# A two-layer decoder trunk on one core: a planner that counts held operand loads, new ranks, and indexer products on 128 rows

## The chip, the core and the metric

The kernel runs on one core of one Trainium2 chip. A core has a matrix engine (PE; its weight loads, PEld, are listed apart), a vector engine (DVE), a scalar engine (ACT), a general engine (POOL), and queues that issue DMA; here SP's queue issues nearly all of them. Each engine runs its instructions in the order in which they were written down and waits on semaphores for the others. The metric is the device time of one execution in microseconds (us).

## What is computed

Two layers, then a final norm, on x of 512 tokens by 1024 channels in float32:

```python
h = rmsnorm(x, norm_w); p = split_cols(h @ w_in)      # w_in: 1024 x 3380
o_a = dsa_mixer(...)   # indexer: 8 heads of 32, relu, weighted sum, top 128 keys; then softmax attention, 4 heads of 64
o_b = nsa_mixer(...)   # compressed blocks, selected blocks and window: three softmaxes, gated
o_c = shortconv_mixer(...); o_d = pool_mixer(...)
mixed = concat(silu(gates) * (o_a, o_b, o_c, o_d))
x = x + mixed @ w_out                                 # after two layers: rmsnorm(x, final_norm_w)
```

The indexer's score of query t and key s is the sum over 8 heads of `relu(qi . ki) * wi`; the compressed branch adds a table `pe_cmp` (32 x 64 per layer) to the tokens of each block before its product.

## The kernel before

Tokens are in four tiles of 128 (`i` = 0 to 3). Every float32 operand of a large product is split into a high part in a rounded format (names `wh`, `hT`, `ph`, `mT` ...) and a rest (`wl`, `pl`, the second `hT` and `mT`), and three products are summed: high by high, high by rest, rest by high. Weights come in parts of 256 rows by up to 384 columns: a DMA into a staging tile `st` (four buffers; two early groups use the tiles `ws`, which are not shared), ACT or DVE writes `wh`, POOL or DVE writes `wl` (`load_w`).

The stages of a layer: `norm_tile` (mean of squares, `pow` on POOL, scaling on DVE, transposes on PE, `hT`); the projections by token tile, `group_a` (360 columns), `group_idx` (256, the indexer's queries `qiT`), `group_bk` (268), `group_bq` (320); `compress`, gates, attention (`att_a`, `att_b`), top-k on DVE (`topk`: 16 pairs of MAX8 and MATCH_REPLACE8 a tile), convolution and pooling, and the output projection (`out_tile`, `store`), whose last column group carries the mean of squares of the next norm.

`group_idx` ends in eight products a tile, `s<-kiT,qiT`: 96 rows hold high, high and rest of the query against high, rest and high of the key. ACT applies relu in the PSUM bank `s` (two banks), DVE adds into `acc`, and a bank is free for the next product when DVE has read it.

Nothing is issued as it is written. Every call is recorded as an `Op` (line 529 of the profile is the one line that later issues them all, so every row of the trace has L529), and `Tape.schedule` puts them in order by list scheduling with its own estimate of each duration (`cost`): for each engine it takes, among the operations that could start soonest, the one whose stage has the lowest number in the table `RANK`; `earliest` says when an operation could start. Queue orders, SP's too, are a result of this. 40 transposes of `ident` at the start (`warm`) are recorded as work with no consumer.

Of the kernel before, what the change touches and what calls it, by code (L numbers as in the profile page):

```python
# [18 lines left out]
P = 128  # L19
T = 512  # L20
# [158 lines left out]
class Op:  # L179
    __slots__ = ("eng", "name", "args", "kw", "outs", "ins", "before", "left", "behind", "dur", "occ", "seen",  # L180
                 "tiles", "start", "ready", "num", "locks", "moves", "stage", "rank", "group", "load", "part")


class Engine:
# [42 lines left out]
class Tape:  # L227
# [37 lines left out]
    def record(self, eng, name, args, kw):  # L265
# [22 lines left out]
        for views, writes in ((op.ins, False), (op.outs, True)):  # L288
            for v in views:
# [3 lines left out]
                if adds:  # L293
                    for (a, b, had), other in v.tile.groups.items():
                        if a == r0 and r1 < b and bits & ~had == 0:
                            op.group = other
                            op.before[other[0].num] = other[0]
                            op.part = True
# [1103 lines left out]
```

## Time and profile before

| | us |
|---|---|
| median of three runs (lowest, highest) | 547.8 (547.03, 548.99) |
| the profiled execution, its own time | 548.15 |
| its span, first to last instruction | 546.4 |
| between the two | 1.75 |

| engine | busy us | share of the span | instructions |
|---|---|---|---|
| PE | 528.5 | 97% | 3139 |
| PEld | 455.9 | 83% | 3139 |
| DVE | 403.9 | 74% | 1139 |
| ACT | 320.7 | 59% | 797 |
| POOL | 320.4 | 59% | 504 |

Busy time of PE is the union of its matmuls, whose ends are modelled and overlap: a PE that is shown busy need not be at its peak, but a PE that is shown idle has nothing. "[2.11 <-ACT wh]" in a row of the timeline is idle time of that engine ahead of the instruction and what ended it. In the views by line, the first number behind the bar is the group's busy time in us, the second the mean of one in ns, the third the idle time ahead of it.

### The profile page before, as it was taken

The numbers are of one execution on the slowest core, as the hardware profiler recorded it, in microseconds if no ns is written. First come the engines' busy times: TensorE is split into PE (matmuls) and PEld (weight loads), VectorE is DVE, ScalarE is ACT, GpSimd is POOL, SyncE is SP. The second block draws the span as 40 slices with busy tenths as digits, with TensorE's granted clock in tenths as the row PEclk, the third lists the DMA queues.
The fourth block names the chain that finished last, engine by engine and source line by source line (L and its number), as shares of the span: only waits on it lengthen the run. The fifth ranks groups of instructions, "written<-read, shape, count | busy, mean of one in ns | idle before, by whom it ended". The sixth has DMA issues, their size and how long they took to land.

```text
span 546.4 us, 9871 instructions
## 1 busy us (share of the span) xinstructions
PE 528.5 (97%) x3139; PEld 455.9 (83%) x3139; DVE 403.9 (74%) x1139; ACT 320.7 (59%) x797; POOL 320.4 (59%) x504
## 2 busy tenths in 40 slices
PE   7979999999999999999999999999999999999995
PEld 7978987677788887899999999777788877788895
DVE  3737799998998878751266568999997968777433
ACT  5358856544486666743255788634366666666433
POOL 6665653373748587636666766347276686574632
PEclk9999999999999999999999999999999999999998
DMA  8761230471224012225642532167142113020304
GB/s 278 195 201 48 50 79 20 130 199 39 60 57 105 3 40 59 78 88 170 191 154 80 132 86 55 39 165 164 40 106 68 50 30 87 0 79 22 104 1 155
DMA packets 70100, 50.65 MB, mean 93 GB/s; under 512 B 19224, under 2 KB 64416, under 8 KB 70048
## 3 DMA queue, kind: packets, MB, share of 16 engines
q1 hardware_dynamic: 69344, 49.38, 32.5%
q10 hardware_dynamic: 704, 0.64, 0.4%
q8 instruction: 25, 0.41, 0.3%
q14 instruction: 27, 0.22, 0.1%
HBM read 45.81 MB, written 4.19 MB: 92 GB/s over the span
## 4 chain that ended last, share of the span: by engine, by line
PE 73%; DVE 9%; DMA 6%; ACT 4%; issue 3%; POOL 3%; SPq 1%; ACTq 0%; POOLq 0%; DVEq 0%
PE mm L529 53%; PE tr L529 8%; PE s L529 6%; PE pv L529 5%; DVE acc L529 4%; DMA st<-in_w_in_dram 3%; ACT wh L529 2%; DVE m L529 2%; POOL pb L529 1%; DMA ws<-in_w_in_dram 1%; POOL wl L529 1%; SPq L529 1%; DMA st<-in_w_out_dram 1%; ACT qiT L529 1%; DVE qb L529 1%
## 5 line engine op out<-in xcount | busy, mean ns | idle before, releaser
L529 POOL TENSOR_TENSOR wl<-st,wh 128x384 fp32r<-128x384 f32 (+4 forms) x188 | 173.5, 952 | 84.3 <-ACT wh L529 69.2
L529 PE MATMUL mm<-hT,wh 128*128 128x512 f32 x544 | 182.2, 403 | 1.4 <-ACT wh L529 1.1
L529 PEld LDWEIGHTS mm<-hT,wh 128*128 128x128 f32 x544 | 100.0, 189 | 20.3 <-ACT wh L529 3.9
L529 PE MATMUL mm<-wh,hT 128*128 128x360 f32 (+3 forms) x480 | 107.0, 308 | 3.0 <-ACT wh L529 2.9
L529 PE MATMUL mm<-hT,wl 128*128 128x512 f32 x272 | 106.8, 403 | 0.0
L529 ACT ACTIVATE wh<-st 128x768 fp32r<-128x768 f32 (+4 forms) x92 | 70.9, 777 | 49.1 <-PE mm L529 25.6
L529 PE MATMUL mm<-wh,mT 128*128 128x384 f32 (+1 forms) x384 | 92.7, 324 | 1.2 <-ACT wh L529 0.5
L529 PEld LDWEIGHTS mm<-wh,hT 128*128 128x128 f32 x480 | 79.5, 189 | 4.8 <-ACT wh L529 3.6
L529 PE MATMUL mm<-wl,hT 128*128 128x360 f32 (+3 forms) x240 | 70.4, 306 | 0.0
L529 PEld LDWEIGHTS mm<-wh,mT 128*128 128x128 f32 x384 | 65.9, 189 | 4.9 <-ACT wh L529 1.2
L529 ACT ACTIVATE pb<-pb,mn 128x512 f32<-128x512 f32 (+3 forms) x96 | 53.3, 557 | 15.1 <-DVE mn L529 14.4
L529 PE MATMUL mm<-wl,mT 128*128 128x384 f32 (+1 forms) x192 | 60.4, 323 | 0.0
L529 PEld LDWEIGHTS mm<-hT,wl 128*128 128x128 f32 x272 | 51.0, 188 | 10.2 <-POOL wl L529 1.8
L529 POOL TENSOR_SCALAR pb<-pb,rs,gt 128x512 f32<-128x512 f32 (+2 forms) x48 | 38.8, 824 | 25.8 <-DVE rs L529 12.2
L529 DVE MATCH_REPLACE8 acc<-m,acc 128x384 f32<-128x384 f32 (+2 forms) x96 | 51.7, 541 | 0.0
L529 ACT ACTIVATE ph<-tr 128x512 fp32r<-128x512 f32 (+1 forms) x68 | 38.1, 595 | 23.2 <-PE tr L529 21.1
L529 DVE MAX8 m<-acc 128x8 f32<-128x384 f32 (+2 forms) x96 | 51.2, 549 | 0.3
L529 DVE TENSOR_TENSOR pl<-tr,ph 128x512 fp32r<-128x512 f32 x60 | 39.9, 684 | 14.6 <-ACT ph L529 11.8
L529 PE MATMUL tr<-ident,pb 128*128 128x128 f32 x240 | 45.7, 275 | 0.9 <-POOL pb L529 0.8
L529 PEld LDWEIGHTS mm<-wl,hT 128*128 128x128 f32 x240 | 44.3, 189 | 0.1
L529 DVE TENSOR_TENSOR x<-mm,x 128x256 f32<-128x256 f32 (+2 forms) x32 | 12.7, 421 | 40.8 <-PE mm L529 40.0
L529 PEld LDWEIGHTS tr<-ident,pb 128*128 128x128 f32 x240 | 30.7, 140 | 10.9 <-POOL pb L529 4.8
(163 smaller groups left out, 915.0 us busy)
## 6 DMA issues: line engine op xcount, KB each, us to landing
st<-in_w_in_dram SPq DMA_DIRECT2D x104, 128.0 KB, 2.6
st<-in_w_in_dram SPq DMA_DIRECT2D x28, 256.0 KB, 2.9
st<-in_w_out_dram SPq DMA_DIRECT2D x16, 384.0 KB, 3.3
x<-in_x_dram SPq DMA_DIRECT2D x16, 256.0 KB, 4.6
st<-in_w_in_dram SPq DMA_DIRECT2D x7, 320.0 KB, 4.6
st<-in_w_out_dram SPq DMA_DIRECT2D x8, 256.0 KB, 2.8
x1d<-x SPq DMA_DIRECT2D x8, 256.0 KB, 3.0
x<-x1d SPq DMA_DIRECT2D x8, 256.0 KB, 2.8
```

The source lines that it names most:

```text
L529: getattr(self.engines[op.eng].real, op.name)(*[real(a) for a in op.args], **{k: real(v) for k, v in op.kw.items()})
```

## The change

- The planner: the field `part` and the rule that let a smaller product join an open accumulation group go. A new field `late` (45 for a transpose, 109 for 128 columns of weights) is added to every wait of a PE operation, on its operands and on its buffers. The spacing of two loads no longer enters `earliest`; it is applied to the operation that was chosen. Some estimates for PE and POOL change.
- `RANK` has new numbers throughout, so the order of every engine changes.
- `group_idx`: the queries are written twice side by side (512 columns instead of 256), rotated twice, and turned by four transposes instead of two; two ACT and two DVE instructions of 64 x 512 write `qiT` in place of eight ACT and four DVE instructions of 32 x 256. The products take 128 rows.
- `mean_sq`: the last column piece of a tile is reduced on DVE (a product and sum with the earlier pieces as its start), where ACT squared and POOL added: 12 pieces in all.
- `compress`: `pe` is loaded turned, by two DMAs of single elements, where a DMA, a PE transpose and an ACT copy made it.
- `pv`: the product with `pl` is one of 512 columns by 128, where it was two of 256 columns by 64; its place is free within the sum. `cmp_pv` and `vc` have 128 rows instead of 96, the added ones zero.

```diff
 RANK = [
-    3, 2, 577, 31, 1, 0, 0, 41, 54, 50, 52, 46, 4, 53, 12, 19, 0, 47, 11, 51, 14, 0, 17, 60, 106, 83, 0, 100, 0,
+    1, 0, 577, 3, 5, 0, 576, 28, 38, 2, 6, 4, 29, 34, 27, 42, 0, 30, 39, 22, 40, 0, 45, 43, 44, 12, 0, 32, 0,
...
                 if adds:
-                    for (a, b, had), other in v.tile.groups.items():
-                        if a == r0 and r1 < b and bits & ~had == 0:
-                            op.group = other
-                            op.before[other[0].num] = other[0]
-                            op.part = True
-                    if op.group is None:
-                        op.group = v.tile.groups.setdefault((r0, r1, bits), [])
-                        if kw["stop"]:
-                            op.before.update((o.num, o) for o in op.group if o.part)
+                    op.group = v.tile.groups.setdefault((r0, r1, bits), [])
...
             op.load = 109 * int(np.prod(op.args[1].shape[1:])) / 128
+            op.late = 45 if op.name == "transpose" else op.load
...
-                        op.occ *= 0.55
+                        op.occ *= 0.6
+                        op.seen += 600
...
-                op.dur = 262 + 0.84 * n
+                op.dur = 262 + 0.84 * n + (75 if sum(isinstance(a, View) for a in op.args) > 3 else 0)
...
-                op.dur = 180 + 2.15 * n
+                op.dur = 180 + (1.7 if len(op.ins) == 2 and op.ins[0].tile is op.ins[1].tile else 2.15) * n
...
-                    s = max(s, pl.free[k])
+                    s = max(s, pl.free[k] + op.late)
                 elif pl.pool.name == "pp":
-                    s = max([s] + [at for other, at in t.used.items() if other != e])
-            if e == "PE" and before is not None:
-                s = max(s, before.start + op.load * (2 if before.start < COLD else 1))
+                    s = max([s] + [at + op.late for other, at in t.used.items() if other != e])
...
             e = op.eng
+            if e == "PE" and last[e] is not None:
+                s = max(s, last[e].start + op.load * (2 if last[e].start < COLD else 1))
...
-                o.ready = max(o.ready, s + (occ if e == "PE" else op.dur + OWN[e]) if o.eng == e else s + op.seen)
+                o.ready = max(o.ready, s + (occ if e == "PE" else op.dur + OWN[e]) if o.eng == e else s + op.seen + o.late)
...
-    def mean_sq(xp, acc):
+    def mean_sq(xp, acc, last=True):
...
-        S.activation(junk[:, : xp.shape[-1]], xp, AF.Square, accum_out=ss)
-        G.tensor_scalar(ss, ss, 1.0 / DM, EPS if acc is None else acc, op0=OP.mult, op1=OP.add)
+        if last and acc is not None:
+            V.tensor_tensor_reduce(out=junk[:, : xp.shape[-1]], in0=xp, in1=xp, scale=1.0 / DM, scalar=acc, op0=OP.mult,
+                                   op1=OP.add, accum_out=ss)
+            return ss
+        S.activation(junk[:, : xp.shape[-1]], xp, AF.Square, scale=DM**-0.5, accum_out=ss)
+        G.tensor_scalar(ss, ss, 1.0, EPS if acc is None else acc, op0=OP.mult, op1=OP.add)
...
-            z = wk.tile([P, 384], F32, name=nm("z"), tag="ph", bufs=3)
-            z3 = z[:, :256].rearrange("p (h d) -> p h d", d=ID)
-            S.activation(z[:, :256], ps[:, :256], AF.Copy)
-            rope(V, z3, IH, 4, tab[:, TB32 + 16 * i : TB32 + 16 * i + 16])
+            z = wk.tile([P, T], F32, name=nm("z"), tag="ph", bufs=3)
+            q3 = ps[:, :256].rearrange("p (h d) -> p h d", d=ID)
+            S.activation(z.rearrange("p (h s d) -> p h s d", s=2, d=ID), q3[:, :, None, :].to_broadcast([P, IH, 2, ID]), AF.Copy)
+            rope(V, z.rearrange("p (h d) -> p h d", d=ID), 2 * IH, 4, tab[:, TB32 + 16 * i : TB32 + 16 * i + 16])
...
-            for h in range(4):
-                src = pq[ID * h : ID * (h + 1), 0 : 2 * P].rearrange("p (b t) -> p b t", b=2)
-                q = qiT[h // 2][:, h % 2]
-                for r in range(2):
-                    S.activation(q[r * ID : (r + 1) * ID], src, AF.Copy)
-                lo(V, q[2 * ID : 3 * ID], src, q[0:ID])
+            for c in range(4):
+                PE.transpose(pq[:, c * P : (c + 1) * P], z[:, c * P : (c + 1) * P], ident)
+            p3 = pq.rearrange("p (c t) -> p c t", c=4)
+            qiT = [wk.tile([P, 4, P], F32R, name=nm("qiT"), tag="big", bufs=BIG) for _ in range(2)]
+            for e in range(2):
+                r, o = slice(HD * e, HD * e + HD), slice(HD - HD * e, P - HD * e)
+                S.activation(qiT[e][r], p3[r], AF.Copy)
+                lo(V, qiT[e][o], p3[r], qiT[e][r])
...
-                PE.matmul(ps[:, :n], qiT[h % 4 // 2][: 3 * ID, h % 2, h // 4, :], kiT[: 3 * ID, :n], start=True, stop=True)
+                PE.matmul(ps[:, :n], qiT[h % 2][:, h // 2, :], kiT[:, :n], start=True, stop=True)
...
-            pet = sm.tile([16, 2, HD], F32, name=nm("pet"), tag="pet", bufs=1)
-            SP.dma_start(pet, pe_cmp[l].rearrange("(s t) d -> t s d", s=2))
-            pt = bank("tr", 3)
-            PE.transpose(pt[:, 0:16], pet.rearrange("t s d -> t (s d)"), ident[0:16, 0:16])
             pe = sm.tile([P, 16], F32, name=nm("pe"), tag="pe", bufs=1)
-            S.activation(pe, pt[:, 0:16], AF.Copy)
+            for s in range(2):
+                SP.dma_start(pe[HD * s : HD * s + HD], pe_cmp[l, 16 * s : 16 * s + 16, :].rearrange("t d -> d t"))
...
-                end = last and k == i
-                if not end:
-                    PE.matmul(po, vt(k), ph, start=first and k == 0, stop=False)
-                if end and i == 0:
-                    PE.matmul(po, vt(k), pl, start=True, stop=False)
-                else:
-                    for c in (slice(0, T // 2), slice(T // 2, T)):
-                        PE.matmul(po[0:HD, c], vt(k)[:, 0:HD], pl[:, c], start=False, stop=False)
-                if end:
-                    PE.matmul(po, vt(k), ph, start=False, stop=True)
+                PE.matmul(po, vt(k), ph, start=first and k == 0, stop=False)
+                PE.matmul(po, vt(k), pl, start=False, stop=last and k == i)
...
-                PE.transpose(pt[0:96, h * P : (h + 1) * P], es[:, h, :], ident)
+                PE.transpose(pt[:, h * P : (h + 1) * P], es[:, h, :], ident)
...
-                    ms[i] = mean_sq(xo, ms[i])
+                    ms[i] = mean_sq(xo, ms[i], e == DM)
```

**Place one: SP's queue in the first 32 us.** `ws_230` before and `ws_216` in the change stage the four parts of the indexer's weights, `ws_254` those of `group_bk`; `x` are token tiles (the later ones for the residual), `pe` and `pet` the table `pe_cmp`. Before, from the last constant to the last part of the indexer's weights:

```order
L529 DMA psc<-in_pool_scale_dram 128x2x1
L529 DMA st_405<-in_w_in_dram 128x2x256
L529 DMA st_405<-in_w_in_dram 128x2x64
L529 DMA pet_426<-in_pe_cmp_dram 16x2x64
L529 DMA ws_230<-in_w_in_dram 128x2x256
L529 DMA g_450<-in_norm_w_dram 128x512
L529 DMA x_461<-in_x_dram 128x512
L529 DMA x_468<-in_x_dram 128x512
L529 DMA x_476<-in_x_dram 128x512
L529 DMA x_484<-in_x_dram 128x512
L529 DMA ws_230<-in_w_in_dram 128x2x256
```

Now, from the last part of the first weights on:

```order
L523 DMA st_189<-in_w_in_dram 128x2x320
L523 DMA st_189<-in_w_in_dram 128x2x40
L523 DMA tab<-in_table_dram 128x258
L523 DMA ws_216<-in_w_in_dram 128x2x256 x4
L523 DMA ws_254<-in_w_in_dram 128x2x268 x4
L523 DMA st_277<-in_w_in_dram 128x2x256
L523 DMA st_277<-in_w_in_dram 128x2x64
L523 DMA pe_290<-in_pe_cmp_dram 64x16x1 x2
```

The indexer's four parts have moved from between the constants and the residual's tiles (the last as SP's 51st DMA) to right behind the table (SP's 16th to 19th).

**Place two: POOL and DVE at the start.** On POOL, the mean of squares of the first token tile (`ss`), the `pow` with `mhalf`, and the rests of the first weights; before:

```order
L529 TENSOR_SCALAR ss_137<-ss_137 128x1
L529 TENSOR_SCALAR ss_163<-ss_163,ss_137 128x1
L529 TENSOR_TENSOR wl_175<-st_90,wh_168 128x360
L529 TENSOR_TENSOR ss_163<-ss_163,mhalf 128x1
L529 TENSOR_TENSOR wl_216<-st_102,wh_186 128x360
```

and now:

```order
L523 TENSOR_SCALAR ss_138<-ss_138 128x1
L523 TENSOR_TENSOR ss_162<-ss_162,mhalf 128x1
L523 TENSOR_SCALAR ss_177<-ss_177 128x1
L523 TENSOR_TENSOR wl_184<-st_87,wh_171 128x360
L523 TENSOR_SCALAR ss_203<-ss_203 128x1
```

The first tile's `pow` has moved ahead of the first `wl`. On DVE in the same stretch (CAST writes `wh`, `xn` is the scaled token tile, ISA the sum of squares and the reading of its accumulator); before:

```order
L529 CAST wh_168<-st_90 128x2x360
L529 TENSOR_TENSOR wl_175<-st_90,wh_168 128x360
L529 CAST wh_186<-st_102 128x2x360
L529 TENSOR_TENSOR wl_216<-st_102,wh_186 128x360
L529 SCALAR_TENSOR_TENSOR xn_232<-x_81,ss_163,s_139 128x512
L529 SCALAR_TENSOR_TENSOR xn_238<-x_92,ss_163,s_154 128x512
L529 CAST wh_263<-st_165 128x2x360
L529 TENSOR_TENSOR hT_273<-tr_240,hT_255 128x4x128
L529 TENSOR_TENSOR hT_273<-tr_253,hT_255 128x4x128
```

and now, behind the first tile's own sum:

```order
L523 CAST wh_171<-st_87 128x2x360
L523 TENSOR_TENSOR wl_184<-st_87,wh_171 128x360
L523 SCALAR_TENSOR_TENSOR xn_199<-x_81,ss_162,s_146 128x512
L523 SCALAR_TENSOR_TENSOR xn_212<-x_89,ss_162,s_156 128x512
L523 ISA junk_223,ss_224<-x_110,ss_177 128x512
L523 ISA ss_224 128x1
L523 ISA junk_238,ss_239<-x_128,ss_203 128x512
L523 ISA ss_239 128x1
L523 TENSOR_TENSOR hT_250<-tr_218,hT_232 128x4x128
L523 TENSOR_TENSOR hT_250<-tr_229,hT_232 128x4x128
L523 CAST wh_268<-st_144 128x2x360
```

The scaled tile comes one weight part earlier, and the second part's `wh` four larger instructions later.

**Place three: DVE at the end,** the last output tiles; before:

```order
L529 TENSOR_TENSOR x_6508<-mm_6822,x_6508 128x256
L529 TENSOR_TENSOR xn_6656<-x_6508,g_6565 128x256
L529 TENSOR_SCALAR xn_6447<-xn_6447,ss_6868 128x512
L529 TENSOR_TENSOR x_3540<-mm_6857,x_3540 128x256
L529 TENSOR_TENSOR xn_6799<-x_3540,g_6565 128x256
L529 TENSOR_SCALAR xn_6603<-xn_6603,ss_6897 128x512
```

and now:

```order
L523 TENSOR_TENSOR xn_6698<-x_3518,g_6430 128x256
L523 TENSOR_SCALAR xn_6466<-xn_6466,ss_6757 128x512
L523 TENSOR_TENSOR x_6396<-mm_6747,x_6396 128x256
L523 ISA junk_6784,ss_6785<-x_6396,ss_6538 128x256
L523 ISA ss_6785 128x1
L523 TENSOR_TENSOR xn_6541<-x_6396,g_6430 128x256
L523 TENSOR_SCALAR xn_6349<-xn_6349,ss_6785 128x512
```

The sum of squares of the last tile has come in between the residual's addition and the product with the norm's weights. The last tile in the order is another one than before, so both its halves leave by SP's queue, where before the second left by ACT's.

## Rows read from the trace of the kernel before

**Rows 1.** Stretches: us, then busy us (and instructions) by engine, clock, DMA.

```profile
0.00:11.40 11.40, 8.56 (x50) 7.93 (x50) 3.71 (x7) 5.63 (x13) 7.01 (x26) 1.00 0.84 263
11.40:31.80 20.40, 20.37 (x131) 19.47 (x132) 15.53 (x38) 10.93 (x32) 12.89 (x30) 1.00 0.74 206
31.80:50.00 18.20, 14.55 (x115) 13.58 (x114) 8.20 (x28) 11.09 (x32) 11.26 (x20) 1.00 0.34 111
50.00:540.30 490.30, 485.02 (x2849) 414.94 (x2847) 375.21 (x1066) 291.78 (x719) 288.42 (x429) 1.00 0.30 82
540.30:546.40 6.10, 0.00 (x0) 0.00 (x0) 1.23 (x3) 1.23 (x3) 0.82 (x2) 0.75 0.46 172
75.00:105.00 30.00, 28.80 (x187) 21.89 (x186) 29.47 (x86) 16.89 (x38) 9.29 (x15) 1.00 0.19 51
```

**Rows 2.** Timeline, 28 to 46 us: start, length, engine, operation, [idle before <-what ended it].

```profile
29.03 0.43 SPq L529 DMA_DIRECT2D ws<-in_w_in_dram  x1
...
31.92 0.42 SPq L529 DMA_DIRECT2D ws<-in_w_in_dram  x1
...
38.46 0.63 ACT L529 ACTIVATE wh<-ws 128x512 fp32r<-128x512 f32 x1 [4.87 <-DMA ws<-in_w_in_dram]
...
39.14 0.51 PE L529 MATMUL mm<-wh,hT 128*128 128x256 f32 x2 [2.11 <-ACT wh L529]
```

**Rows 3.** Timeline, 0 to 14 us, the first token tile.

```profile
5.47 0.27 POOL L529 TENSOR_SCALAR ss<-ss,ss 128x1 f32<-128x1 f32 x1 [0.72 <-ACT junk L529]
...
7.78 0.54 DVE L529 CAST wh<-st 128x720 fp32r<-128x720 f32 x1 [4.29 <-DMA st<-in_w_in_dram]
...
8.40 1.30 POOL L529 TENSOR_TENSOR wl<-st,wh 128x360 fp32r<-128x360 f32 x1 [2.67 <-DVE wh L529]
...
9.67 0.85 POOL L529 TENSOR_TENSOR ss<-ss,mhalf 128x1 f32<-128x1 f32 x1
...
10.58 1.40 DVE L529 SCALAR_TENSOR_TENSOR xn<-x,ss,s 128x512 f32<-128x512 f32 x2
...
12.72 0.43 PE L529 MATMUL mm<-wh,hT 128*128 128x360 f32 x1
...
12.99 1.28 DVE L529 TENSOR_TENSOR hT<-tr,hT 128x512 fp32r<-128x512 f32 x2
```

**Rows 4.** By line and shape: xcount | busy us, mean ns | idle before; sums of squares.

```profile
L529 DVE CUSTOM_DVE_ANT_0 pb<-s,mask 128x512 f32<-128x512 f32 x16 | 10.8, 683 | 0.1
...
L529 DVE CUSTOM_DVE_ANT_0 pb<-s,mask 128x256 f32<-128x256 f32 x16 | 6.7, 417 | 1.5 <-PE s L529 1.5
```

**Rows 5.** By line and shape: the indexer's products, and attention's of like columns.

```profile
L529 PE MATMUL s<-kiT,qiT 96*128 96x512 f32 x16 | 7.1, 446 | 0.0
...
L529 PE MATMUL s<-kTA,qa 128*128 128x512 f32 x16 | 5.4, 417 | 0.1
...
L529 PE MATMUL s<-kiT,qiT 96*128 96x256 f32 x16 | 5.5, 341 | 0.6 <-ACT qiT L529 0.6
...
L529 PE MATMUL s<-kTA,qa 128*128 128x256 f32 x16 | 2.9, 293 | 0.0
```

**Rows 6.** Timeline, 28 to 46 us: three transposes of a projection.

```profile
33.80 0.49 PE L529 MATMUL tr<-ident,z 128*128 128x128 f32 x3
```

**Rows 7.** By line and shape: products with the probabilities' rest and high part.

```profile
L529 PE MATMUL pv<-pl,vB 128*64 128x256 f32 x80 | 17.3, 300 | 0.0
...
L529 PE MATMUL pv<-ph,vB 128*128 128x512 f32 x40 | 15.9, 406 | 0.0
```

**Rows 8.** Timeline, from 540 us to the end: the last output tile.

```profile
540.72 0.42 ACT L529 ACTIVATE junk<-x 128x256 bf16<-128x256 f32 x1 [0.60 <-DVE x L529]
...
541.33 0.27 POOL L529 TENSOR_SCALAR ss<-ss,ss 128x1 f32<-128x1 f32 x1 [1.97 <-ACT junk L529]
...
541.67 0.55 POOL L529 TENSOR_TENSOR ss<-ss,mhalf 128x1 f32<-128x1 f32 x1
...
543.01 0.37 ACTq L529 DMA_DIRECT2D out_dram<-xn  x1
```

More of the change, by code (lines that the diff above doesn't have):

```diff
@@ L180 @@
     __slots__ = ("eng", "name", "args", "kw", "outs", "ins", "before", "left", "behind", "dur", "occ", "seen",
-                 "tiles", "start", "ready", "num", "locks", "moves", "stage", "rank", "group", "load", "part")
+                 "tiles", "start", "ready", "num", "locks", "moves", "stage", "rank", "group", "load", "late")
 class Engine:
@@ L277, in record @@
         op.group = None
-        op.part = False
         op.behind = []
@@ L333, in cost @@
         op.locks = False
-        op.load = 0.0
+        op.load = op.late = 0.0
         op.moves = op.eng in ("ACT", "DVE") and len({v.region()[0] for v in op.outs[:1] + tensors}) > 1
@@ L690, in trunk @@
     psh = const.tile([P, DEPTH, 2], F32, name="psh")
-    e_split = [const.tile([P, NH, 96], F32, name=f"es{s}") for s in range(2)]
+    e_split = [const.tile([P, NH, P], F32, name=f"es{s}") for s in range(2)]
     for t_ in e_split:
-        G.memset(t_[:, :, HD:96], 0.0)
+        G.memset(t_[:, :, HD:P], 0.0)
     x1d = dp.tile([T, DM], F32, name="x1d")
@@ L739, in rms @@
             for b in range(2):
-                ms = mean_sq(xt[b], ms)
+                ms = mean_sq(xt[b], ms, b == 1)
         G.tensor_tensor(ms, ms, mhalf, OP.pow)
@@ L761, in rope @@
         r = 2 * half
-        t1 = sm.tile([P, 9, 16], F32, name=nm("r1"), tag="r1", bufs=2)
-        t2 = sm.tile([P, 9, 16], F32, name=nm("r2"), tag="r2", bufs=2)
-        t1, t2 = t1[:rows, :n, :r], t2[:rows, :n, :r]
+        t1, t2 = (sm.tile([P, 144], F32, name=nm(t), tag=t, bufs=2) for t in ("r1", "r2"))
+        t1, t2 = (t[:rows, : n * r].rearrange("p (n r) -> p n r", r=r) for t in (t1, t2))
         def bc(a, m):
@@ L813, in group_idx @@
             yield
-            z = wk.tile([P, 384], F32, name=nm("z"), tag="ph", bufs=3)
-            z3 = z[:, :256].rearrange("p (h d) -> p h d", d=ID)
-            S.activation(z[:, :256], ps[:, :256], AF.Copy)
-            rope(V, z3, IH, 4, tab[:, TB32 + 16 * i : TB32 + 16 * i + 16])
+            z = wk.tile([P, T], F32, name=nm("z"), tag="ph", bufs=3)
+            q3 = ps[:, :256].rearrange("p (h d) -> p h d", d=ID)
+            S.activation(z.rearrange("p (h s d) -> p h s d", s=2, d=ID), q3[:, :, None, :].to_broadcast([P, IH, 2, ID]), AF.Copy)
+            rope(V, z.rearrange("p (h d) -> p h d", d=ID), 2 * IH, 4, tab[:, TB32 + 16 * i : TB32 + 16 * i + 16])
             yield
             pq = bank("tr", 3)
-            for b in range(2):
-                PE.transpose(pq[:, b * P : (b + 1) * P], z[:, b * P : (b + 1) * P], ident)
-            qiT = [wk.tile([P, 2, 2, P], F32R, name=nm("qiT"), tag="big", bufs=BIG) for _ in range(2)]
-            for h in range(4):
-                src = pq[ID * h : ID * (h + 1), 0 : 2 * P].rearrange("p (b t) -> p b t", b=2)
-                q = qiT[h // 2][:, h % 2]
-                for r in range(2):
-                    S.activation(q[r * ID : (r + 1) * ID], src, AF.Copy)
-                lo(V, q[2 * ID : 3 * ID], src, q[0:ID])
+            for c in range(4):
[6 more added lines that the diff above has]
+                lo(V, qiT[e][o], p3[r], qiT[e][r])
             yield
@@ L948, in layer @@
             G.memset(f(kTB[s][:, 0, 0:32]), 0.0)
-        vc = res.tile([96, P], F32R, name=nm("vc"), tag="vc")
-        G.memset(f(vc[HD:96]), 0.0)
+        vc = res.tile([P, P], F32R, name=nm("vc"), tag="vc")
+        G.memset(f(vc[HD:P]), 0.0)
         @tape.staged
@@ L1190, in cmp_pv @@
             for h in range(NH):
-                PE.transpose(pt[0:96, h * P : (h + 1) * P], es[:, h, :], ident)
+                PE.transpose(pt[:, h * P : (h + 1) * P], es[:, h, :], ident)
             ph = wk.tile([P, T], F32R, name=nm("ph"), tag="ph", bufs=3)
-            S.activation(ph[0:96], pt[0:96], AF.Copy)
-            PE.matmul(po, vc, ph[0:96], start=False, stop=True)
+            S.activation(ph, pt, AF.Copy)
+            PE.matmul(po, vc, ph, start=False, stop=True)
         def cd(s="cd"):
```

53 rows, old and new, of the table RANK are left out of this document.

## The prediction

> **What bounds the kernel now.** I read the stretches first: is any engine full, and where is it not? PE is shown busy 8.56 of the first 11.40 us (idle transposes for the most part, since the first product starts at 12.72), 20.37 of the next 20.40, 14.55 of the next 18.20, 485.02 of the next 490.30, and not at all in the last 6.10 [rows 1, 3]. So all idle time of PE is 2.84 + 0.03 + 3.65 + 5.28 + 6.10 = 17.9 us of 546.4. PE is the bound from 12.72 to 540.3 us, and the kernel can be made faster in three ways only: less work for PE, less of that idle time, and less time that a product spends on a weight load that came late, which the stretches show as busy. DVE is nearly full in one place, 29.47 of 30.00 us between 75 and 105 us, where top-k begins, and PE has 1.2 us of idle time there [rows 1].
>
> Then I read the timeline where PE idles most, and ask what ended the wait. Between 31.8 and 50 us it is one cause: SP issues the last two parts of the indexer's weights at 29.03 and 31.92 us, ACT splits the last at 38.46 after 4.87 us of waiting for that DMA, and PE, idle for 2.11 us, goes on at 39.14 [rows 2]. Nothing held these DMAs but the instructions queued ahead of them. Last the start, the shapes of the products, and the end [rows 3 to 8].
>
> The profiled execution took 548.15 us, its span 546.4; 1.75 us lie outside. I make the sum against it. It stands 0.35 us above the median of 547.8, so I take 0.35 off at the end. A measurement of this kernel tells about 0.3%, 1.6 us, from no change.
>
> **The change part by part.**
>
> *Start, to the first products.* The first tile's mean of squares was on POOL by 5.47 + 0.27 = 5.74 us, but its pow stood behind a `wl` of 1.30 us that waited for weights, and ran at 9.67; the scaling followed at 10.58 [rows 3]. In the new order the pow comes first, and DVE can scale behind the first CAST and `wl`, at 7.78 + 2 x 0.55, about 8.9 us: 1.7 us earlier. But then DVE has two more sums of squares at 0.68 (nearest row: the 512-column reduction of attention) and two `hT` in 1.28 before the second part's CAST: 8.9 + 1.40 + 2 x 0.76 (0.08 for each accumulator read, my allowance) + 1.28 + 0.54 = 13.6 us [rows 3, 4]. Until then PE has only the six products of the first part that are written ahead, and before the change dense work began at 12.72. I take 0; bounds -1.6 (the early start is kept) and +1.5 (DVE, now with nine more short steps in its queue before all tiles are normalized, is late for the next parts too).
>
> *The hole at 32 to 39 us.* The four parts now follow the table, without x tiles or constants between; SP issued the table at the eleventh microsecond before, and needs some 0.45 us for each DMA [rows 2], so all four are out by about 15 us instead of 32. Next late is what is left: a few short waits for keys, some 0.6 us. I take -3.65 + 0.6 = -3.0; bounds -3.65 and 0.
>
> *Indexer's products.* Queries on 128 rows cost PE the same columns. The 48 products before were longer than attention's with as many columns, 446 against 417 ns at 512 and 341 against 293 at 256: 29 and 48 ns, 38 between for 384, 16 of each: 1.8 us [rows 5]. I read this as the load that waited for its bank or operand, which the planner now counts. Half of it: -0.9; bounds -1.8 and 0. ACT loses 36 instructions net here, beside PE's other products; it matters only if ACT is late for them, and it costs nothing either way as long as PE has projections to run.
>
> *More transposes.* Twelve more of 128 columns. Three took 0.49 us, 0.16 each with the last one's drain [rows 6]: 12 x 0.16 = 2.0 us at most, 0 at least (their loads beside long products). I take +1.2. The two of `pe` that go are worth -0.3.
>
> *Rest of the probabilities.* 58 products of 512 columns in place of 116 of 256. Two halves are 2 x 17.3/80 = 0.43 us, one whole 15.9/40 = 0.40 [rows 7]; 58 x 0.035 = 2.0 us at most, but much of a half's time is drain under the next one, and the columns are the same. I take -0.5; bounds -2.0 and 0.
>
> *Loads of `pe`, `cmp_pv`, memsets.* The two DMAs of single elements are SP's 26th and 27th and are needed by POOL only in `compress`, after all projections; I cost them at nothing. If that cover went, they would hold up the parts of the last projection's weights behind them. 128 rows instead of 96 are the same columns and loads.
>
> *The end.* Last tile: ACT 0.42 at 540.72, POOL 0.27 at 541.33, pow 0.55 at 541.67, last DMA issued at 543.01 [rows 8]. A DVE reduction of 256 columns takes 0.42 [rows 4] and saves the POOL step and two passings between engines: 541.67 becomes about 541.2, -0.45. Against it, both last stores now stand in SP's queue, some 0.4 us of issue, and only the later of the two counts. I take -0.3; bounds -0.45 and +0.1.
>
> The trace shows one thing on POOL beside DVE: the pow that ran while DVE was casting and subtracting took 0.85 us, the last one, alone, 0.55 [rows 3, 8]. The Trainium skill, "SBUF — State Buffer", section "Who interferes with whom", says that a DVE instruction with two inputs in SBUF shuts out a POOL instruction that reads SBUF until it is done. By that rule the last tile's product with the norm's weights (two SBUF inputs, now right behind the reduction) would hold its pow for most of 0.42 us, and the end would gain 0.1 instead of 0.45; the trace agrees as far as those two rows go.
>
> *The rest of the order.* Every stage from 50 us on has new ranks. Its visible idle time is 5.28 us [rows 1]: at best all of it goes, at worst it doubles. The counted loads argue for a gain, as at the indexer; I take -1.0.
>
> Sum: 0 - 3.0 - 0.9 + 1.2 - 0.3 - 0.5 - 0.3 - 1.0 = -4.8. 548.15 - 4.8 = 543.35, less 0.35: **543.0 us**.
>
> **The rivals.**
>
> *The hole only moves.* DVE's longer queue at the start holds up the second to fourth weight parts, PE waits in pieces at 13 to 30 us instead of once at 37, and the new ranks, made for the planner's estimates, bring nothing later (a change in what the planner counts need not change what the chip waits for). For it: every `hT`, half the CASTs and now the sums stand in one DVE queue, and DVE was busy 15.53 of 20.40 us there [rows 1]. Against: 20.37 of 20.40 us of PE were filled in the same stretch. -4.8 + 3.0 + 1.0 gives -0.8: 547.0.
>
> *Slower: top-k starves attention.* PE comes 3 us earlier to the stage at 75 us, where DVE has 0.5 us of slack in 30 [rows 1]. DVE's pairs of MAX8 and MATCH_REPLACE8 are in one queue with the minima and rests of attention; if those are ranked behind top-k steps, PE uses up its gates and projections and waits for the first attention block. Then the start's 3.0 us come back as waiting, and the visible idle time after 50 us doubles: -4.8 + 3.0 + 1.0 + 5.3 = +4.5, 552.3. It decides for slower once idle time between 50 and 540 us exceeds 5.28 by some 2.5 us more than the early start gains back. Against it: 485 of 490 us were filled by the same mix of work.
>
> *All bounds good.* The early start is kept (-1.6), the hole goes whole (-3.65), all 1.8 us at the indexer, and 3 of the 5.28 us: with +1.2, -0.3, -0.5 and -0.3 that is -10.0: 537.8.
>
> **How the numbers follow.** Forecast 0.60, the hole moves 0.16, top-k starves attention 0.12, all bounds good 0.12. Around the forecast the unknown terms (start, rest of the order, transposes) make about 538.5 to 547. Of the two outer cases I leave out most of the slow one and half of the good one: range 538.5 to 549.0. Below 546.2 lie the forecast, the good case and a little of the second: faster 0.73; within 0.3% most of the second and the forecast's upper edge: 0.14; slower 0.13.
>
> **What would show it.** Between the first product and 50 us PE should be idle for about 1 us in all, where the hole alone was 3.65, and no row of ACT waiting several us for the indexer's weights; the first product should start near 11 us. The indexer's products should average near 417 and 293 ns. The pow of the last tile should follow its sum within 0.2 us, or be held by the DVE product. Wrong is the prediction if PE's idle time between 50 and 540 us is well above 5 us, if idle time appears at 13 to 30 us, or if the time moves with PE's idle time unchanged.

## The result, and the profile after

The changed kernel takes 540.81 us in the median (539.79 to 542.12), the kernel before 548.37 (547.03 to 548.99) beside it: a ratio of 0.9862, 95% interval 0.9845 to 0.9879. It is 7.6 us faster; 543.0 was forecast, with a range of 538.5 to 549.0. The profiled execution has a span of 538.8 us, where before it was 546.4.

The stretches of the kernel after (us, then busy us and instructions of PE, PEld, DVE, ACT, POOL, then clock, DMA share, GB/s) stand against [rows 1]:

```profile
0.00:11.40 11.40, 8.51 (x51) 7.79 (x52) 3.92 (x10) 3.97 (x8) 6.36 (x26) 1.00 0.80 251
11.40:31.80 20.40, 19.54 (x130) 18.67 (x129) 16.92 (x43) 10.31 (x28) 11.99 (x19) 1.00 0.92 245
31.80:50.00 18.20, 14.87 (x104) 13.98 (x103) 7.87 (x30) 9.37 (x28) 10.95 (x22) 0.91 0.30 78
50.00:532.90 482.90, 480.27 (x2811) 419.04 (x2811) 379.99 (x1069) 277.12 (x673) 288.02 (x425) 1.00 0.31 83
532.90:538.80 5.90, 0.00 (x0) 0.00 (x0) 1.74 (x5) 0.72 (x1) 0.67 (x1) 0.76 0.47 178
75.00:105.00 30.00, 29.58 (x193) 23.44 (x193) 29.59 (x88) 18.44 (x41) 11.64 (x18) 1.00 0.26 58
```

The surprise is the third row. The hole was to go, and PE is still idle for 18.20 - 14.87 = 3.33 us there, and its clock is 0.91, where it was 1.00. The fourth row has the gain that can be seen at once: 2.63 us of idle time over 483 us, where it was 5.28. From the first product to the end of the last one it is 521.06 us (11.80 to 532.86), before 527.44 (12.72 to 540.16). So 0.9 us lie ahead of the first product, 6.4 between, and 0.3 behind. Of the 6.4, PE's idle time between the first and the last product explains 2.0 (8.8 before, 6.8 after); the rest is in time that the page shows as busy.

It can be seen where PE's weight loads wait. The waits of PEld from 50 us on, before (us in total, times, the longest):

```profile
PEld mm L529 <- ACT wh L529: 5.4, 12, 1.6
PEld s L529 <- DVE acc L529: 5.2, 21, 0.5
PEld tr L529 <- POOL pb L529: 4.8, 15, 0.7
PEld mm L529 <- POOL wl L529: 2.1, 7, 0.5
```

and after:

```profile
PEld s L523 <- DVE acc L523: 3.7, 10, 1.1
...
PEld tr L523 <- POOL pb L523: 2.1, 8, 0.4
PEld mm L523 <- ACT wh L523: 1.3, 5, 0.4
...
PEld mm L523 <- POOL wl L523: 0.9, 5, 0.3
```

Waits for `wh` fell from 5.4 to 1.3 us, for `pb` from 4.8 to 2.1, for `wl` from 2.1 to 0.9. I also counted them from the starts of the products. A load is late when it waited at least 40 ns and the two spacings around it are together at least 50 ns above those of undisturbed products (231 ns at 512 columns, 174 at 384, 147 at 320, 118 at 256). From 45 us on, 101 loads were late before, with 23.9 us above those spacings, idle time included; after, 67 with 15.2 us. That is 8.7 us, a little more than the whole gain. A narrower count, of loads for which the trace names what ended the wait, gives 88 with 20.8 us and 51 with 12.0: 8.8 us. It is a count of where the time shows; whether late loads set the time is asked further down.

### The profile page after: what moved, and what is told of

Its sections match the earlier page's. It is cut to its first block, busy times and chain, and to the rows that moved or that the text cites. A ratio compares the mean times of both kernels' runs of the same rounds, so it can differ in the third digit from the quotient of the medians.

```text
span 538.8 us, 9722 instructions
## 1 busy us (share of the span) xinstructions
PE 523.2 (97%) x3091; PEld 459.5 (85%) x3091; DVE 410.4 (76%) x1151; ACT 301.5 (56%) x735; POOL 318.0 (59%) x492
## 4 chain that ended last, share of the span: by engine, by line
PE 78%; DVE 11%; DMA 4%; issue 3%; POOL 1%; ACT 1%; SPq 0%; ACTq 0%; POOLq 0%; DVEq 0%
PE mm L523 57%; PE tr L523 10%; PE s L523 6%; PE pv L523 6%; DVE acc L523 5%; DMA st<-in_w_in_dram 3%; DVE m L523 2%; POOL wl L523 1%; DVE qb L523 1%; DMA x<-in_x_dram 1%; DVE qiT L523 1%; SPq L523 0%; ACT qiT L523 0%; ACT wh L523 0%; DMA cw<-in_conv_w_dram 0%
## 5 line engine op out<-in xcount | busy, mean ns | idle before, releaser
L523 POOL TENSOR_TENSOR wl<-st,wh 128x384 fp32r<-128x384 f32 (+4 forms) x188 | 177.9, 974 | 79.2 <-ACT wh L523 63.2
L523 PE MATMUL mm<-wh,hT 128*128 128x360 f32 (+3 forms) x480 | 108.6, 310 | 0.5 <-ACT junk L523 0.5
L523 PE MATMUL mm<-wh,mT 128*128 128x384 f32 (+1 forms) x384 | 90.2, 321 | 0.4 <-DVE x L523 0.4
L523 PE MATMUL mm<-wl,hT 128*128 128x360 f32 (+3 forms) x240 | 73.2, 311 | 3.1 <-POOL wl L523 3.1
L523 ACT ACTIVATE pb<-pb,mn 128x128 f32<-128x128 f32 (+3 forms) x96 | 53.3, 557 | 17.9 <-DVE mn L523 17.4
L523 ACT ACTIVATE ph<-tr 128x512 fp32r<-128x512 f32 x68 | 38.1, 595 | 29.0 <-PE tr L523 22.4
L523 DVE MAX8 m<-acc 128x8 f32<-128x512 f32 (+2 forms) x96 | 51.4, 550 | 0.5
L523 DVE MATCH_REPLACE8 acc<-m,acc 128x512 f32<-128x512 f32 (+2 forms) x96 | 51.7, 541 | 0.0
L523 POOL TENSOR_SCALAR pb<-pb,rs,gt 128x512 f32<-128x512 f32 (+2 forms) x48 | 33.7, 715 | 20.7 <-DVE rs L523 6.6
```

The source lines that it names most:

```text
L523: getattr(self.engines[op.eng].real, op.name)(*[real(a) for a in op.args], **{k: real(v) for k, v in op.kw.items()})
```

## Experiments: the gap at 34 us

The timeline of the kernel after, 31 to 41 us (start, length, engine, operation, idle time before and what ended it):

```profile
32.25 0.59 SPq L523 DMA_DIRECT2D cw<-in_conv_w_dram  x1
...
34.06 0.59 SPq L523 DMA_DIRECT2D psc<-in_pool_scale_dram  x1
...
34.62 0.20 POOL L523 TENSOR_SCALAR cwh<-cw 128x12 f32<-128x12 f32 x1 [7.92 <-DMA cw<-in_conv_w_dram]
...
36.50 0.20 POOL L523 TENSOR_SCALAR psh<-psc 128x4 f32<-128x4 f32 x1 [1.68 <-DMA psc<-in_pool_scale_dram]
36.66 2.79 POOL L523 TENSOR_TENSOR wl<-ws,wh 128x256 fp32r<-128x256 f32 x4
...
37.44 0.49 PE L523 MATMUL mm<-wl,hT 128*128 128x256 f32 x1 [3.13 <-POOL wl L523]
```

To be read from below: PE waits 3.13 us for a `wl`. POOL makes it at 36.66, right behind `psh`, which waited for the DMA of `psc`; before that POOL had stood for 7.92 us at `cwh`, a halving of 12 columns that waits for `cw`. Both constants are needed only in the convolution and the pooling, much later. Before the change the last DMA of `cw` was issued 7.3 us earlier, and `cwh` ran at 27.26 us:

```profile
24.91 0.59 SPq L529 DMA_DIRECT2D cw<-in_conv_w_dram  x1
...
27.26 0.20 POOL L529 TENSOR_SCALAR cwh<-cw 128x12 f32<-128x12 f32 x1 [2.34 <-DMA cw<-in_conv_w_dram]
```

What has passed the constants in SP's queue? Of the indexer's four parts only two: in the trace of before they are issued at 12.28, 16.30, 29.03 and 31.92 us, so two stood ahead of the constants already, and place one above is wrong where it lets all four come from behind them. Beside these two, two tiles of `x`, two parts in `st` and the two DMAs of `pe` have passed. Those of `pe` took 2.7 us of SP's time, and the pair of `st` behind them 2.83, where the pair at 24.20 takes 0.89; the first of it waited until POOL was done at 22.39 (the kernel after):

```profile
17.57 2.60 SPq L523 DMA_DIRECT2D pe<-in_pe_cmp_dram  x2
...
20.28 2.83 SPq L523 DMA_DIRECT2D st<-in_w_in_dram  x2
```

So the first experiment takes the two small instructions out of POOL's way:

```diff
         order = self.schedule()
+        small = [op for op in order if op.outs and op.outs[0].tile.name in ("cwh", "psh")]
+        order = [op for op in order if op not in small]
+        at = next(k for k, op in enumerate(order) if self.stages[op.stage] == "gates")
+        order[at:at] = small
```

> The changed kernel, in which two small POOL instructions (the halving of the convolution's and the pooling's constants, cwh and psh) are taken out of POOL's queue ahead of the indexer's weight rests and put behind compress. Theory 'hole' (the stretch without products at 34.3 to 37.4 us comes from these two, which wait for their DMAs with the rests queued behind them, and the low clock after it comes from the stretch): PE's 3.1 us of idle time go and about 18 products of 256 columns run at 118 instead of 213 ns, 1.7 us; about 536 us where the kernel before takes 548.4, a ratio near 0.977. Rival (the rests are paced by POOL itself at 0.7 us each, so PE waits anyway): about 1 us goes, ratio near 0.9845, and idle time stays at 34 to 38 us.

Measured: 536.25 us, ratio 0.9768 (0.9736 to 0.9800). The `wl` are made from 29.27 us on, and PE has no gap. The same two stretches, in the kernel after and in this one:

```profile
34.30:37.40 3.10, 0.01 (x1) 0.00 (x0) 0.50 (x2) 0.47 (x1) 1.10 (x4) 1.00 0.56 154
37.40:41.10 3.70, 3.66 (x16) 3.46 (x16) 0.00 (x0) 0.00 (x0) 3.70 (x8) 0.54 0.78 234
```

```profile
34.30:37.40 3.10, 3.10 (x28) 3.10 (x28) 0.69 (x4) 1.42 (x5) 3.10 (x8) 1.00 0.82 196
37.40:41.10 3.70, 3.70 (x34) 3.69 (x33) 2.27 (x11) 2.18 (x8) 0.67 (x1) 1.00 0.54 193
```

The gap has a price of its own behind it: for 3.7 us the granted clock is 0.54, nearly all at the lower of the two levels, 1.2 GHz, and 16 products ran where 34 did at 1.00. Their starts are 213 ns apart instead of 118, 16 x 0.095 = 1.5 us. With the 3.1 us of the gap that is 4.6; the ratios differ by 0.0094, 5.2 us, with an uncertainty of some 2. Theory 'hole' holds. No other kernel here is clearly faster.

Was the hole of the kernel before really due to the late weights, as I had read [rows 2]? There the four DMAs alone were moved:

```diff
+        parts = [op for op in order if op.name == "dma_start" and op.outs and op.outs[0].tile.place.tag == "mT0"]
+        order = [op for op in order if op not in parts]
+        at = next(k for k, op in enumerate(order) if op.name == "dma_start" and op.outs and op.outs[0].tile.name == "tab")
+        order[at + 1 : at + 1] = parts
```

> The kernel before, its order kept, in which only the four DMAs of the indexer's weights are moved in SP's queue to right behind the table. Theory of the forecast (PE's 3.65 us of idle time there come from these late DMAs alone): 3.0 us less, ratio near 0.9945. Rival (the conv constants' DMAs are put back by the four, and POOL, which halves them ahead of the weight rests, waits for them instead): the idle time only moves, ratio 0.998 to 1.002, with POOL waiting for cw longer than the 2.3 us of before.

Measured: 547.37 us, ratio 0.9983 (0.9964 to 1.0003): about 0.9 us of the 3.0, and no change at all lies within the interval, as the rival has it. The timeline of this kernel shows the rival's wait, and what PE waits for behind it:

```profile
29.08 0.20 POOL L533 TENSOR_SCALAR cwh<-cw 128x12 f32<-128x12 f32 x1 [3.80 <-DMA cw<-in_conv_w_dram]
30.84 0.20 POOL L533 TENSOR_SCALAR psh<-psc 128x4 f32<-128x4 f32 x1 [1.57 <-DMA psc<-in_pool_scale_dram]
...
34.72 0.55 PE L533 MATMUL tr<-ident,z 128*128 128x128 f32 x3 [1.49 <-POOL z L533]
```

`cwh` waits 3.80 us where it waited 2.34, and runs 1.8 us later than before. That is what the indexer's parts alone do to it; in the changed kernel it runs 7.4 us later, so most of that delay comes from the other DMAs that passed the constants, `pe` among them. No run moves those by themselves. The rotation of `z` is queued behind it, and PE waits for `z` instead of for `wh`. With both moves, the DMAs and the two POOL instructions:

> The kernel before, its order kept but for two moves: the four DMAs of the indexer's weights right behind the table, and the halving of the conv and pool constants on POOL behind compress. Theory 'one queue behind another' (the late DMAs and POOL's wait for the conv constants stand in for each other, so that only both together free PE): 3.0 to 3.65 us less than before, ratio 0.9935 to 0.9945. Rival (PE waits there for something third): ratio 0.997 or more.

Measured: 546.63 us, ratio 0.9962 (0.9944 to 0.9979), 2.1 us less than before. In the profile the stretch from 31.8 to 50 us has 0.53 us of idle time left:

```profile
31.80:50.00 18.20, 17.67 (x141) 16.93 (x140) 11.75 (x34) 13.65 (x41) 13.39 (x22) 1.00 0.43 123
```

and 0.65 more at 11.4 to 31.8. So most of the hole goes, if both queues are cleared; 3.68 - 1.18 = 2.5 us won at the place are 2.1 (1.2 to 3.1) at the end. That lies between the two expectations. The POOL move alone was not run in the kernel before.

## Experiments: parts and order

Here the order of every engine is kept as the kernel's own planner makes it, and only when an instruction is issued does another stand in its place. First the product with the probabilities' rest, in the kernel before:

```diff
-                        PE.matmul(po[0:HD, c], vt(k)[:, 0:HD], pl[:, c], start=False, stop=False)
+                        op = PE.matmul(po[0:HD, c], vt(k)[:, 0:HD], pl[:, c], start=False, stop=False)
+                        tape.whole[op.num] = None if c.start else (po, vt(k), pl)
```

> The kernel before, its order kept, in which only the product with the probabilities' rest is changed: one of 512 columns by 128 in the place of the first half, none in the place of the second. Theory 'order' (the change's gain lies in the order of PE's work, so that fewer weight loads wait): 0 to 1 us less, ratio 0.998 to 1.000. Rival 'parts' (the gain lies in the parts that are rewritten): 2 us less or more, ratio at most 0.996.

Measured: 549.15 us, ratio 1.0008 (0.9989 to 1.0028). No effect. Then the sums of squares, back to the old way in the changed kernel:

```diff
+            if op.name == "tensor_tensor_reduce" and op.outs[0].tile.name.startswith("junk"):
+                o = {k: real(v) for k, v in op.kw.items()}
+                self.engines["ACT"].real.activation(o["out"], o["in0"], AF.Square, scale=DM**-0.5, accum_out=o["accum_out"])
+                self.engines["POOL"].real.tensor_scalar(o["accum_out"], o["accum_out"], 1.0, o["scalar"], op0=OP.mult, op1=OP.add)
+                continue
```

> The changed kernel, its order kept, in which only the last piece of each mean of squares is back on ACT and POOL, in the place of the DVE reduction. Theory 'order': 0.3 us more at the end and little elsewhere, ratio to the kernel before 0.986 to 0.988. Rival 'parts': 2 us more or over, ratio 0.990 or more.

Measured: 542.67 us, ratio 0.9894 (0.9865 to 0.9922); that is between the two expectations, and the intervals overlap a little, so the 1.8 us more than the changed kernel takes have an uncertainty of nearly as much. Of it 0.16 us lie behind the last product (6.10 us to the end instead of 5.94). Another part is at the passage between the layers, where PE now waits for the scaled tile, and in the kernel after doesn't wait at all (PE's waits from 255 to 290 us of this kernel):

```profile
PE tr L528 <- DVE xn L528: 0.9, 2, 0.7
```

The indexer's transposes, each issued a second time in the changed kernel:

```diff
+            if op.name == "transpose" and self.stages[op.stage] == "group_idx":
+                self.engines["PE"].real.transpose(*[real(a) for a in op.args])
```

> The changed kernel with each of the 24 transposes of the indexer's queries issued twice, so 24 more where the change added 12. The forecast's term (0.1 us each, bounds 0 and 0.16): 2.4 us more than the changed kernel (0 to 3.9), ratio to before 0.9906. Rival (their loads lie beside long products and cost PE nothing): ratio 0.986.

Measured: 541.61 us, ratio 0.9878 (0.9861 to 0.9895): 0.9 us more for 24, with the intervals overlapping. A transpose costs 0.04 us here, and between 0 and 0.1.

Then all parts at once, both ways round. The new parts in the order of before (doubled queries, whole products, sums on DVE; in this order three of the first layer's four sums start from the earlier piece before POOL has scaled it, with the same instructions, so this kernel's result is wrong there and only its time is used):

```diff
+            tape.instead.update((at + k, []) for k in range(12))
+            for e in range(2):
+                r, o = slice(HD * e, HD * e + HD), slice(HD - HD * e, P - HD * e)
+                Listed("ACT", new).activation(qn[e][r], p3[r], AF.Copy)
+                lo(Listed("DVE", new), qn[e][o], p3[r], qn[e][r])
+            tape.instead.update({at: new[:1], at + 2: new[1:2], at + 6: new[2:3], at + 8: new[3:]})
...
-            getattr(self.engines[op.eng].real, op.name)(*[real(a) for a in op.args],
-                                                        **{k: real(v) for k, v in op.kw.items()})
+            for eng, name, args, kw in self.instead.get(op.num, [(op.eng, op.name, op.args, op.kw)]):
+                getattr(self.engines[eng].real, name)(*[real(a) for a in args], **{k: real(v) for k, v in kw.items()})
```

> The kernel before, planned as before and issued in its order; only when it is issued do the rewritten parts stand in the places of the old ones: doubled queries with four transposes, two ACT and two DVE instructions, products on 128 rows, whole products with the rest, the last piece of each mean of squares on DVE. Theory 'order' (the gain lies in where things stand in the queues): within 1.5 us of before, ratio 0.997 to 1.003. Rival 'parts' (it lies in ACT's and POOL's saved instructions): 3 to 6 us less, ratio 0.989 to 0.995.

Measured: 549.31 us, ratio 0.9993 (0.9978 to 1.0008). The parts alone bring nothing, as theory 'order' says. In its trace the first product starts at 14.29 us, 1.57 later than before, with a DVE sum now ahead of the first scaled tile, and from there to the end of the last one it takes 526.51 us, 0.93 less. And the old parts in the new order, by the same means:

> The changed kernel, planned and ordered as it is; only when it is issued do the old parts stand in the places of the rewritten ones: queries by two transposes, eight ACT and four DVE instructions, products on 96 rows, halved products with the rest (but where one opens or closes its sum), the last piece of the mean of squares on ACT and POOL. Theory 'order': 1 to 2.5 us are lost, most of it the sums (1.7 us when they alone were put back), ratio to before 0.988 to 0.991. Rival 'parts': 4 us or more are lost, ratio 0.993 or more.

Measured: 554.43 us, ratio 1.0086 (1.0068 to 1.0104). Not 1 to 2.5 us are lost but 12.3 (0.0224 x 548.4), and the kernel is slower than before. So theory 'order' falls too, as I had put it: the new order alone is worse than the old one. The last run puts only the queries back:

> The changed kernel, planned and ordered as it is; only the indexer's queries are made and used in the old way when it is issued (copy of 256 columns, two transposes, eight ACT and four DVE instructions a tile, products on 96 rows). With all three old parts in this order 13.6 us were lost, 1.7 of them by the sums. Theory 'fit' (the new order counts on the short way to the queries): 9 to 12 us are lost here alone, ratio to before 1.002 to 1.008. Rival (the halved products with the rest cost them, or only all parts together): 0 to 4 us, ratio 0.986 to 0.994.

Measured: 553.81 us, ratio 1.0087 (1.0053 to 1.0121). As far as the intervals tell (some 2 us), the whole loss is in the queries' way; by the ratios it is 12.3 us, a little over the 9 to 12 of theory 'fit'. In its trace ACT's and DVE's instructions for a tile are these (by line and shape: xcount | busy us, mean ns):

```profile
L533 ACT ACTIVATE qiT<-tr 32x256 fp32r<-32x256 f32 x48 | 18.0, 375 | 0.6
...
L533 DVE TENSOR_TENSOR qiT<-tr,qiT 32x256 fp32r<-32x256 f32 x24 | 10.1, 421 | 9.9 <-ACT qiT L533 9.5
```

where the kernel after has

```profile
L523 DVE TENSOR_TENSOR qiT<-tr,qiT 64x512 fp32r<-64x512 f32 x12 | 8.3, 689 | 1.9 <-ACT qiT L523 1.6
...
L523 ACT ACTIVATE qiT<-tr 64x512 fp32r<-64x512 f32 x12 | 7.1, 589 | 0.1
```

For each of the six tiles ACT needs 8 x 0.375 = 3.0 us instead of 2 x 0.589 = 1.2, and the first product of the indexer waits for `qiT` by as much (PE's waits of the kernel with the old queries, 45 to 60 us):

```profile
PE s L533 <- DVE qiT L533: 1.8, 1, 1.8
```

PE has projections left while it waits. They stand behind the indexer's product in its queue, and run as soon as it has started:

```profile
51.20 0.39 PE L533 MATMUL s<-kiT,qiT 96*128 96x256 f32 x1 [1.82 <-DVE qiT L533]
51.42 0.53 PE L533 MATMUL mm<-wh,hT 128*128 128x268 f32 x2
```

The stretches of this kernel in which the two layers' indexers run, and the same of the kernel after:

```profile
50.00:75.00 25.00, 22.13 (x147) 20.68 (x148) 16.68 (x48) 19.46 (x55) 14.72 (x29) 0.93 0.23 57
300.00:350.00 50.00, 44.72 (x300) 42.30 (x299) 35.87 (x107) 33.96 (x96) 27.51 (x56) 0.93 0.32 78
```

```profile
50.00:75.00 25.00, 24.77 (x181) 23.87 (x181) 20.86 (x57) 16.01 (x44) 17.61 (x37) 1.00 0.33 82
300.00:350.00 50.00, 48.81 (x325) 44.26 (x325) 43.72 (x123) 33.78 (x83) 28.03 (x56) 1.00 0.33 80
```

PE is idle for 2.87 + 5.28 = 8.15 us instead of 0.23 + 1.19 = 1.42, which is 6.7 us more. And its clock is 0.93, where it was 1.00: if that is the mean of the two levels over the 75 us, 0.07 x 75 = 5.3 us of work at the full clock were not done. Together 12.0 us, where some 12.3 were lost. That the two agree so well is partly chance: over the whole trace PE's idle time between the first and the last product grew by 9.5 us, which with the clock makes 14.7, and the span from the first to the last product grew by 14.3.

One more run gives the program of the changed kernel to the planner and the table of before:

> The program of the changed kernel with the planner and the table of the kernel before (both have 616 stages, so that the table can be read). Theory 'order': a table fits only the program and the planner it was made with; slower than before by 1 to 6%, ratio 1.01 to 1.06. Rival 'parts': faster than before, ratio 0.99 or less.

Measured: 580.17 us, ratio 1.0550 (1.0523 to 1.0578). This table doesn't carry over: with this program it costs 30.7 us against the kernel before. A table for the old parts from the new planner, or for the new planner without `late`, was not made. So what the counting of held loads is worth by itself stays open.

| | order of before | order of after |
|---|---|---|
| parts of before | 1 | 1.0086 |
| parts of after | 0.9993 | 0.9862 |

## Experiments: late loads pulled ahead of

If late loads are 8.7 us, can they be mended one by one? In the kernel before, at 81 of the late loads, a later product whose operands were there was pulled ahead:

```diff
+        for k, j in AHEAD:
+            at = {op.num: n for n, op in enumerate(order)}
+            order.insert(at[j], order.pop(at[k]))
```

> The kernel before, in which at 81 places a product whose operands are there already is pulled ahead of one whose weight load was held by a wait in the trace; nothing else is touched. Theory 'order' (a load held by a wait costs PE some 0.1 us or more, and what a product in its place covers is won): 3 to 6 us less, ratio 0.989 to 0.9945, and clearly fewer held loads. Rival 'pace' (the engines that produce the operands set the pace, and what is won at one place is waited for at the next): 0 to 1 us less, ratio 0.998 or more.

Measured: 548.4 us, ratio 1.0000 (0.9982 to 1.0018). The waits of PEld from 50 us on are those of before, nearly:

```profile
PEld mm L545 <- ACT wh L545: 5.6, 10, 1.5
PEld s L545 <- DVE acc L545: 4.6, 18, 0.4
PEld tr L545 <- POOL pb L545: 4.2, 13, 0.7
```

At the 81 places the spacings around the two products were 21.7 us above the undisturbed ones before and 16.4 here: 5.3 us were won there, but over all products from 45 us on it is 47.8 and 47.3. What is won at one place is waited for at the next, as 'pace' says (though at some of the 81 the product pulled ahead waited for the same weights, so the test is weaker there). The same at 49 places in the changed kernel, with the two POOL instructions behind `compress`:

> The changed kernel with the two small POOL instructions behind compress (as in the run that had only this, ratio 0.9768) and with 49 products pulled ahead of products whose weight load was held in its trace. Theory 'order': 1.5 to 3.5 us less than with the POOL move alone, ratio 0.970 to 0.974. Rival 'pace': the same as with the POOL move alone, 0.976 to 0.978.

Measured: 535.56 us, ratio 0.9775 (0.9750 to 0.9799), the same as without it (0.9768). By these two runs a late load is where the pace of ACT, DVE and POOL shows; it isn't what sets it.

## Why the prediction was right, and where it wasn't

The time lies in the range, and the direction is right, but two large terms were both wrong, in opposite directions, and the sum hides it: that it came within 2.2 us is luck. By its steps (the span went from 546.4 to 538.8, -7.6 us):

| step | forecast | measured |
|---|---|---|
| start | 0 | first product 0.92 earlier, 0.83 more idle time before 31.8 us: -0.1 (first products in the new order start between 10.67 and 11.87 us from trace to trace) |
| hole at 32 to 39 us | -3.0 | idle time -0.3, low clock behind it +1.5: +1.2 |
| indexer's late loads | -0.9 | 0 |
| twelve transposes | +1.2 | +0.4 (half of the run with 24) |
| two transposes of `pe` | -0.3 | not measured apart |
| loads of `pe` | 0 | 2.7 us of SP's queue ahead of the constants; their share of the hole not measured apart |
| rest of the probabilities | -0.5 | 0 (+0.4, -0.6 to +1.5, in the old order) |
| end | -0.3 | -0.3 |
| rest of the order | -1.0 | what remains, the parts' fit to it included: about -8.8 |

**The hole.** The step that failed is "next late is what is left: a few short waits for keys, some 0.6 us". The four DMAs themselves came early, as forecast: they had landed by 18.3 us. But I asked what they wait for, and not who waits for the DMAs that are passed in the queue. Those of `cw` and `psc` feed POOL instructions that stand ahead of the weight rests. It could have been seen in the order and in the trace of before, where `cwh` waited for `cw` already. A second step failed with it: "I cost them at nothing", of the two DMAs of `pe`. I looked at when `pe` is needed and not at what SP's queue holds behind it. They took 2.7 us ahead of the constants, nearly the length of PE's gap; how much of the gap is theirs no run shows. The rival 'the hole only moves' came true in this, by another mechanism than mine (DVE's queue, 13 to 30 us). What my list of signs called wrong (idle time at 13 to 30 us) was there only as 0.83 us.

**The queries.** "It costs nothing either way as long as PE has projections to run" agrees with the order of before (0.9993 with all three new parts). In the new order the condition is met and the step still fails: PE has projections to run, but they stand behind the indexer's product in its queue, and it doesn't run them while it waits. The short way is worth 12 us there. My sum took the parts one by one against the old order, where together they are worth nothing.

**The rest of the order.** Mis-sized from -1.0 to about -8.8. I let only the visible idle time of 5.28 us count, "at best all of it goes". But a late load mostly costs time that the page shows as busy: 23.9 us lay in late loads, with idle time in it. Only 2.65 of the 8.8 is idle time that went. My last sign of being wrong, the time moving with PE's idle time unchanged, came true for the larger part of the gain. The table of parts and order shows that neither brings it alone; which of the new ranks bring it stays open.

**The indexer's products.** I expected them near 417 and 293 ns. The groups of the kernel after, against [rows 5]:

```profile
L523 PE MATMUL s<-kiT,qiT 128*128 128x512 f32 x16 | 7.2, 449 | 0.9 <-DVE acc L523 0.9
...
L523 PE MATMUL s<-kiT,qiT 128*128 128x384 f32 x16 | 6.7, 419 | 0.2 <-DVE acc L523 0.2
...
L523 PE MATMUL s<-kiT,qiT 128*128 128x256 f32 x16 | 5.0, 324 | 0.2 <-DVE qiT L523 0.2
```

7.2 + 6.7 + 5.0 = 18.9 us, before 19.0. They wait for DVE's `acc` to free one of two banks, beside top-k, where DVE is busy for 29.59 of 30.00 us. So the half of their excess that I took off did not go.

**The end.** 6.28 us from the last product to the end of the span became 5.94, and the sum follows [rows 8]:

```profile
533.47 0.48 DVE L523 CUSTOM_DVE_ANT_0 junk<-x,ss 128x256 bf16<-128x256 f32 x1
533.88 0.08 DVE L523 DVE_READ_ACCUMULATOR2_ANT ss<- 128x1 f32 x1
533.88 0.42 DVE L523 TENSOR_TENSOR xn<-x,g 128x256 f32<-128x256 f32 x1
534.04 0.67 POOL L523 TENSOR_TENSOR ss<-ss,mhalf 128x1 f32<-128x1 f32 x1 [2.21 <-DVE ss L523]
534.74 0.49 DVE L523 TENSOR_SCALAR xn<-xn,ss 128x512 f32<-128x512 f32 x1 [0.44 <-POOL ss L523]
```

The `pow` starts while DVE's product with two inputs is running and takes 0.67 us, where it took 0.55 alone: 0.12 us. The Trainium skill, "SBUF — State Buffer", section "Who interferes with whom", would hold it until the product is done, at 534.30, so that it ended at 534.85; it ended at 534.71. The direction agrees, the size is about half (a span on POOL is rough).

## What to carry to other kernels

When a transfer is moved forward in a queue, list the transfers that it passes, find the instruction that waits for each of them, and read what is queued behind that instruction on its engine; count the issue time of small transfers in that queue too. A halving of twelve columns held up PE for 3 us here. Cost a shorter chain in the order that it will stand in; the same parts were worth 0 us in one order and 12 in the other, so parts and order have to be judged together. And a late weight load hides in busy time: compare product spacings with undisturbed ones before taking the idle time for all that an order can win, and don't expect to mend such loads one at a time.

## What was not expected of the hardware

The clock fell behind short gaps, and not always. Before the change PE was idle for 2.11 us at 37 to 39 us, and the clock of the stretch stayed at 1.00 [rows 1, 2]; after it, 3.13 us of idle time were followed by 3.7 us at 0.54. The run with the old queries has a gap of 1.8 us, and the clock fell behind it:

```profile
49.30:51.20 1.90, 0.08 (x2) 0.01 (x1) 0.45 (x2) 1.84 (x6) 0.73 (x2) 1.00 0.00 0
51.20:55.60 4.40, 4.40 (x23) 4.40 (x24) 2.96 (x8) 4.26 (x12) 1.74 (x2) 0.61 0.22 52
```

while the run with all old parts has the same gap at the same place and keeps its clock:

```profile
51.00:55.60 4.60, 4.59 (x37) 4.59 (x38) 2.98 (x8) 4.46 (x12) 1.74 (x2) 1.00 0.26 64
```

23 products ran in 4.4 us there, 37 in 4.6 here. Nor does the length of the gap decide it alone: with the transposes issued twice, 2.10 us of idle time at 34 us were followed by 3.4 us at 0.57, where the 2.11 before the change were not. So a gap near 2 us may cost as much again behind it, or nothing.
